# Three transformer blocks on one core: block 1's attention without GpSimd, modulation steps moved, tiles padded to aligned places

## The chip, the cores and the metric

The kernel runs on one core of one Trainium2 chip. The metric is the device time of one execution in microseconds (us). A core has five engines with an instruction queue each, and each works through its queue in order: TensorE (PE, matrix products, with its weight loads shown apart as PEld), VectorE (DVE), ScalarE (ACT), GpSimd (POOL) and SyncE (SP), which here only starts transfers. Transfers run on 16 DMA engines. On-chip memory is SBUF (128 partitions, operands) and PSUM (128 partitions, results of PE).

## The reference

One sequence of 1024 tokens of width 1024 goes through three blocks. The first is the one whose code changes most:

```
h = rmsnorm(x, g_in);  proj = h @ w_in          # q, k, v, u, b, c, q_mem, gate
# sticks-breaking attention, 8 heads of 64:
z = q k^T / 8
A[t,s] = sigmoid(z[t,s]) * prod_{s<j<t} (1 - sigmoid(z[t,j]))     for s < t
y_sb = A v
y_conv = b * causal_conv3(c * u)
y_mem = softmax attention over 256 memory tokens (rmsnorm(mem) @ w_mem_kv)
x = x + (concat(norms of y_sb, y_conv, y_mem) * silu(gate)) @ w_out;  rmsnorm
```

Block 2 modulates its input with six vectors, `ada = silu(c) @ w_ada + b_ada` (a 1024 x 6144 matrix), then mixes with a gated recurrence (HGRN2) and a spatial gating unit, and runs a mixture of 32 experts. Block 3 has 16 more tokens in front, a convolution of width 31 beside a latent attention, and a feed-forward layer of width 2816. All of it is in 32-bit floats.

## The kernel before

Every large product is made of three PE products: each operand is split into a rounded high part (`hi`, cast on ACT, L70) and the rest (`lo`, a subtraction on DVE, L71, on POOL in places), and `mm3` (L76 to L78) adds hi x hi, lo x hi and hi x lo in PSUM. Weights come 128 x 1024 at a time on SP's queue, and are split after landing.

Block 1 runs in stages. The value projection `vproj` comes first, then `heads(0)`, the query and key projections of the first pair of heads. Attention is four passes, j = 0 to 3, of one pair of heads each; a pass has eight query blocks i of 128 rows. For block i, `scores` makes z for both heads in PSUM with n = 128 (i+1) columns; ACT makes 1 - sigmoid (`nb`) and sigmoid (`be`); DVE runs a product scan along the row, backwards (`nb`, L294); POOL multiplies `be` by the shifted scan (L296) after a one-column memset (L293). `attend` then, one block later, transposes the weights on PE (L309), copies them from PSUM to `wt`, on DVE and ACT in turns (L313), and multiplies them with the values (`pv`, L320). After blocks 0, 2, 4 and 6 PE does one half-projection of the next pair of heads (`heads(j + 1)`). At the head of a pass the queries and keys are split (`qs` L85 on DVE, `kk` L93 on POOL). After attention come the convolution (six projections of two halves each, L250 evacuates a half on DVE), the memory attention, the gates, and the output projection.

Modulation of block 2 runs as a background task. One step (`background`) loads a 128 x 512 piece of `w_ada`, 256 KB (L680), and accumulates it on DVE (L711, `acc`); 96 steps make twelve vectors of 512, and after each vector two or eight matmuls close it (L692, L698). `nbg` gives the number of steps before and after each `attend`, 24 for a pass, 96 in all; the loads share SP's queue with the weights, in three buffers, two of them loaded in advance from the head of the program.

The order of each engine's queue is made by the framework's scheduler from the program's order and the buffers, and tiles get their SBUF addresses from pools, one behind the other, so a tile's start address follows from the sizes of the tiles before it.

## Time and profile before

| | us |
|---|---|
| median of three runs (lowest, highest) | 3194.37 (3192.73, 3198.25) |
| the profiled execution, its own time | 3193.8 |
| span in the profile | 3192.1 |
| PE busy, share of the span | 2938.7, 92% |
| DVE busy | 1948.9, 61% |
| ACT busy | 1170.4, 37% |
| POOL busy | 847.8, 27% |

The span reaches from the first to the last recorded instruction; the execution's own time lies 1.7 us above it. Busy times of engines overlap, since the engines run beside each other. In the trace attention lies between about 102 and 391 us, the convolution from 391 to about 460, memory attention and gates up to 619, the output projection to 728, block 2's mixers to about 1245, experts to about 1900, and block 3 to the end, with the feed-forward layer from about 2540.

### The profile page before, as it was taken

What the parts mean: (1) busy time and instruction counts of PE and PEld (TensorE: products, weight loads), DVE (VectorE), ACT (ScalarE), POOL (GpSimd) and SP (SyncE); (2) the same over time, 40 slices, a digit from 0 to 9 for tenths busy, and PEclk for the clock granted to TensorE, in tenths of its full rate; (3) what the DMA queues carried; (4) which work ended last, traced back from release to release, by engine and by line L of the source; (5) the groups of instructions that cost most, each with busy time, mean ns of one, the idle gap of its engine ahead of it and who ended that gap; (6) DMA issues with size and microseconds to landing.
All of it is one profiled execution on the core that took longest, in us unless ns stands there. A gap on an engine that the chain in (4) does not pass through costs nothing. (4 is left out here: it accounts for less than half of the span.)

```text
span 3192.1 us, 47341 instructions
## 1 busy us (share of the span) xinstructions
PE 2938.7 (92%) x18630; PEld 2520.0 (79%) x18630; DVE 1948.9 (61%) x2753; ACT 1170.4 (37%) x2006; POOL 847.8 (27%) x618
## 2 busy tenths in 40 slices
PE   6978799998989886899999599999999999999998
PEld 6755587778777774777777599866699999999997
DVE  5688855662664577564876679786644544444445
ACT  3444426532554212342554443346414222222222
POOL 0333421000544454232433201100103222222221
PEclk9998899999999997899999799999999999999999
DMA  6122221222110244656886511400022111111111
GB/s 221 40 93 92 85 64 62 90 80 70 34 35 21 67 146 165 205 170 196 268 275 225 163 47 49 129 21 21 9 93 68 40 55 50 48 47 40 47 47 60
DMA packets 97038, 298.23 MB, mean 93 GB/s; under 512 B 13556, under 2 KB 17396, under 8 KB 96648
## 3 DMA queue, kind: packets, MB, share of 16 engines
q1 hardware_dynamic: 82200, 246.21, 22.6%
q0 software_dynamic: 8784, 31.99, 4.1%
q10 hardware_dynamic: 5792, 16.54, 1.6%
q8 instruction: 165, 2.70, 0.3%
q14 instruction: 97, 0.79, 0.1%
HBM read 254.61 MB, written 40.08 MB: 92 GB/s over the span
## 5 line engine op out<-in xcount | busy, mean ns | idle before, releaser
L71 DVE TENSOR_TENSOR w_lo<-w_raw,w_hi 128x1024 fp32r<-128x1024 f32 (+3 forms) x134 | 157.6, 1178 | 303.5 <-ACT w_hi L70 303.2
L78 PE MATMUL psu<-f_hi,w_lo 128*128 128x342 f32 x1056 | 337.1, 319 | 0.6 <-DVE w_lo L71 0.6
L70 ACT CAST w_hi<-w_raw 128x1024 fp32r<-128x1024 f32 (+3 forms) x156 | 148.7, 955 | 514.6 <-PE ps L77 179.1
L76 PE MATMUL psu<-f_hi,w_hi 128*128 128x342 f32 x1056 | 337.1, 319 | 0.0
L77 PE MATMUL psu<-f_lo,w_hi 128*128 128x342 f32 x1056 | 337.1, 319 | 0.0
L78 PEld LDWEIGHTS psu<-f_hi,w_lo 128*128 128x128 f32 x1056 | 198.8, 188 | 0.8 <-DVE w_lo L71 0.8
L77 PEld LDWEIGHTS psu<-f_lo,w_hi 128*128 128x128 f32 x1056 | 198.8, 188 | 0.4
L76 PEld LDWEIGHTS psu<-f_hi,w_hi 128*128 128x128 f32 x1056 | 198.6, 188 | 0.4
L1419 DVE TENSOR_TENSOR wlo<-raw,whi 128x1024 fp32r<-128x1024 f32 x120 | 192.8, 1671 | 7.1 <-ACT whi L1365 5.6
L1365 ACT CAST whi<-raw 128x1024 fp32r<-128x1024 f32 x156 | 155.4, 1048 | 49.3 <-DMA raw<-in_w_down 25.1
L1779 DVE SCALAR_TENSOR_TENSOR u<-u,conv_w 128x1040 f32<-128x1040 f32 x120 | 159.9, 1332 | 6.5 <-ACT u L1777 5.1
L77 PE MATMUL ps<-wlo,xhi 128*128 128x512 f32 x400 | 158.0, 395 | 6.2 <-DVE wlo L1419 5.8
L76 PE MATMUL ps<-whi,xhi 128*128 128x512 f32 x400 | 158.0, 395 | 4.6 <-issue 3.1
L78 PE MATMUL ps<-whi,xlo 128*128 128x512 f32 x400 | 157.4, 394 | 0.0
L76 PE MATMUL ps<-hhi,w_hi 128*128 128x512 f32 x384 | 154.3, 402 | 0.0
L77 PE MATMUL ps<-hlo,w_hi 128*128 128x512 f32 x384 | 152.7, 398 | 0.0
L78 PE MATMUL ps<-hhi,w_lo 128*128 128x512 f32 x384 | 152.1, 396 | 0.0
L131 POOL TENSOR_TENSOR w_raw<-w_raw,ffn_norm_g 128x1024 f32<-128x1024 f32 x44 | 87.1, 1982 | 222.8 <-DMA w_raw<-in_w_up 215.8
L2217 DVE TENSOR_TENSOR acc<-acc,psd 128x512 f32<-128x512 f32 x176 | 116.1, 683 | 43.2 <-PE psd L78 41.7
L77 PE MATMUL psd<-w_lo,a_hi 128*128 128x512 f32 x352 | 139.4, 396 | 1.3 <-POOL w_lo L71 1.3
L78 PE MATMUL psd<-w_hi,a_lo 128*128 128x512 f32 x352 | 139.3, 396 | 0.0
L76 PE MATMUL psd<-w_hi,a_hi 128*128 128x512 f32 x352 | 139.1, 396 | 0.0
(614 smaller groups left out, 8071.2 us busy)
## 6 DMA issues: line engine op xcount, KB each, us to landing
raw<-in_w_up SPq DMA_DIRECT2D x104, 512.0 KB, 5.3
w_raw<-in_w_in SPq DMA_DIRECT2D x54, 512.0 KB, 3.7
raw<-in_w_down SPq DMA_DIRECT2D x52, 512.0 KB, 3.9
w<-in_w_ada SPq DMA_DIRECT2D x96, 256.0 KB, 2.8
w_raw<-in_w_up SPq DMA_DIRECT2D x44, 512.0 KB, 3.6
w_raw<-in_w_down SPq DMA_DIRECT2D x22, 512.0 KB, 3.6
w_raw<-in_w_out SPq DMA_DIRECT2D x16, 512.0 KB, 6.5
xk<-in_xT SPq DMA_DIRECT2D x16, 256.0 KB, 6.9
```

Source lines behind the costliest of these rows:

```text
L70: (hi_eng or nc.scalar.copy)(hi, v)
L71: (lo_eng or nc.vector).tensor_sub(lo, v, hi.bitcast(F32))
L76: mm(out, l[0], r[0], start=start, stop=False)
L77: mm(out, l[0], r[1], start=False, stop=False)
L78: mm(out, l[1], r[0], start=False, stop=stop)
L131: nc.gpsimd.tensor_mul(w, w, gain[:, :, None].to_broadcast(sh))
L1365: nc.scalar.copy(self.whi[j], self.raw[j % NR])
L1419: lambda j, *w: (nc.gpsimd if j in (4, 7) else nc.vector).tensor_sub(*w))
L1779: keep(nc.vector.scalar_tensor_tensor(acc, x, w, acc, op0=OP.mult, op1=OP.add))
L2217: nc.vector.tensor_add(acc[t][:, ns], acc[t][:, ns], ps)
```

## The change

Four things change.

- In attention, POOL has no work. DVE multiplies `be` by the scan (L298, one column less, so that no memset is needed) and subtracts for `kk` (L93); ACT makes all copies to `wt` and the zeros of the memory keys.
- `background` is called from other places and takes a number of steps: three for each of the second value projection's row blocks, four after each half-projection of the convolution, two at each half of the gates, the rest at the end. The first loads start after the last value weights instead of at the head; four buffers instead of three.
- The memory tokens are loaded and split (`memory()`) after the first of the convolution's two column groups, not after the convolution.
- Tiles are padded or share a place ("room", "edge", rows of 1152, 1120, 1056 or T + 16 instead of odd lengths). Of the tiles in SBUF 860 of 2404 began at a multiple of 64 bytes before and 2139 of 2400 do now; at a multiple of 512 bytes 287 and now 1461. All 512-column matmuls now read both operands from multiples of 512 bytes; before, only some did: the experts' operands did, `w_hi` of block 1's projections began 384 bytes past one, the down-projection's operands 96 and 128 past, block 2's projections 32 past. The feed-forward chunks become 352, 336 and 338 columns instead of three of 342, in rows of T + 16.

```diff
@@ pair_double
-            self.nc.gpsimd.tensor_sub(lo[h][own], x[own], hi[h][own].bitcast(F32))
+            self.nc.vector.tensor_sub(lo[h][own], x[own], hi[h][own].bitcast(F32))
@@ vproj, and what follows the second half's weights
                     nc.scalar.activation(vt[:, t, g * 256:(g + 1) * 256], ps[:, :256], AF.Copy,
                                          scale=rt[:, t:t + 1])
+                    background(psm, 3 * g)
...
                 wvpart(1, w1, c)
+            background(psm, 0)
@@ proj
-        def proj(m, outs, scale=1.0):
+        def proj(m, outs, scale=1.0, steps=0):
             w = ws.load(a["w_in"][m])
             for hf in range(2):
                 proj_half(w, hf, outs[hf], scale)
+                background(psm, steps)
@@ scores
-                    nb = at.tile([P, T + 1], F32, name="nb", bufs=2)
+                    nb = at.tile([P, T], F32, name="nb", bufs=2)
...
-                    nc.gpsimd.memset(nb[:, n:n + 1], 1.0)
                     nc.vector.tensor_tensor_scan(nb[:, :n][:, ::-1], nb[:, :n][:, ::-1],
                                                  nb[:, :n][:, ::-1], 1.0, op0=OP.mult, op1=OP.bypass)
-                    nc.gpsimd.tensor_mul(be[:, :n], be[:, :n], nb[:, 1:n + 1])
+                    nc.vector.tensor_mul(be[:, :n - 1], be[:, :n - 1], nb[:, 1:n])
@@ attend
-                        eng = nc.scalar.copy if cx.flip % 2 else nc.vector.tensor_copy
-                        cx.flip += 1
-                        eng(wt[:, c * P:(c + nbk) * P], pt[:, :nbk * P])
+                        nc.scalar.copy(wt[:, c * P:(c + nbk) * P], pt[:, :nbk * P])
@@ the passes
                     scores(j, i)
-                    nbg = (0, 0, 1, 2, 2, 2, 2, 3)[i]
-                    for _ in range(nbg):
-                        background(psm)
                     if len(todo) == 1:
                         attend(*todo.pop(0))
                     todo.append((j, i))
-                    for _ in range(nbg):
-                        background(psm)
...
-            background(psm, last=True)
@@ convolution
-                proj(12 + j, halves(u))
-                proj(16 + j, halves(c))
-                proj(14 + j, halves(b))
+                proj(12 + j, halves(u), steps=4)
+                proj(16 + j, halves(c), steps=4)
+                proj(14 + j, halves(b), steps=4)
...
+                if j == 0:
+                    memory()
@@ gates
-                    yield gate(m, hf, gate_of(pl, w, hf))
+                    gt = gate_of(pl, w, hf)
+                    background(psm, 2)
+                    yield gate(m, hf, gt)
...
+            background(psm, 0, last=True)
@@ ada
-                w = pl.tile([P, 512], F32, name="w", bufs=3)
+                w = pl.tile([P, 512], F32, name="w", bufs=4)
...
-        for _ in range(2):
+        for _ in range(3):
             load()
...
-                g = pl.tile([P, 512], F32, name="g", bufs=1)
+                g = pl.tile([P, 512], F32, name="g", tag="w", bufs=4)
@@ placement, a few of many
-    FCH = ((0, 342), (342, 342), (684, 342))
+    FCH = ((0, 352), (352, 336), (688, 338))
...
-        self.fhi = fp.tile([P, 8, T + 2], F32R, name="f_hi")
+        self.fhi = fp.tile([P, 8, T + 16], F32R, name="f_hi")[:, :, :T + 2]
...
+        self.cv.tile([P, 88], F32, name="room")
...
+        edge = es.enter_context(tc.tile_pool(name="edge", bufs=1, side="right")).tile([P, 120], F32, name="edge")
```

What this does to the queues, at three places. First DVE ahead of attention, from the end of the input statistics to the first evacuation of a head's projection. In each row stands the line, the operation, result and operands, the shape, and a count where rows repeat. `wvl` and `w_lo` are weight splits, `kk` zeros. Before:

```order
L711 SCALAR_TENSOR_TENSOR acc<-w,cs,acc 128x512 x4
L71 TENSOR_TENSOR wvl_136<-w_raw,wvh_135 128x1024
L711 SCALAR_TENSOR_TENSOR acc<-w,cs,acc 128x512
L71 TENSOR_TENSOR wvl_136<-w_raw,wvh_135 128x1024
L711 SCALAR_TENSOR_TENSOR acc<-w,cs,acc 128x512 x3
L71 TENSOR_TENSOR w_lo<-w_raw,w_hi 128x1024
L711 SCALAR_TENSOR_TENSOR acc<-w,cs,acc 128x512
L71 TENSOR_TENSOR w_lo<-w_raw,w_hi 128x1024
L711 SCALAR_TENSOR_TENSOR acc<-w,cs,acc 128x512 x7
L273 TENSOR_SCALAR kk<-ones 64x1024 x2
L250 SCALAR_TENSOR_TENSOR x<-ps,rb 128x512
```

The same stretch of DVE's queue after the change (the steps are now L718, evacuations L252):

```order
L718 SCALAR_TENSOR_TENSOR acc<-w,cs,acc 128x512 x3
L71 TENSOR_TENSOR wvl_131<-w_raw,wvh_130 128x1024 x2
L718 SCALAR_TENSOR_TENSOR acc<-w,cs,acc 128x512 x4
L71 TENSOR_TENSOR w_lo<-w_raw,w_hi 128x1024
L718 SCALAR_TENSOR_TENSOR acc<-w,cs,acc 128x512
L71 TENSOR_TENSOR w_lo<-w_raw,w_hi 128x1024
L718 SCALAR_TENSOR_TENSOR acc<-w,cs,acc 128x512 x16
L276 TENSOR_SCALAR kk<-ones 64x1024 x2
L718 SCALAR_TENSOR_TENSOR acc<-w,cs,acc 128x512 x7
L252 SCALAR_TENSOR_TENSOR x<-ps,rb 128x512
L718 SCALAR_TENSOR_TENSOR acc<-w,cs,acc 128x512
```

There were 16 steps ahead of the first evacuation; now there are 31, and one behind it.

Second, DVE in attention, in query blocks 5 to 7 of a pass (the scan is printed as SCALAR_TENSOR_TENSOR on `nb`). Before:

```order
L294 SCALAR_TENSOR_TENSOR nb<-nb 128x768
L313 COPY wt<-ps 128x512
L294 SCALAR_TENSOR_TENSOR nb<-nb 128x768
L313 COPY wt<-ps 128x512
L294 SCALAR_TENSOR_TENSOR nb<-nb 128x896
L313 COPY wt<-ps 128x512
L294 SCALAR_TENSOR_TENSOR nb<-nb 128x896
L313 COPY wt<-ps 128x512
L711 SCALAR_TENSOR_TENSOR acc<-w,cs,acc 128x512 x6
L250 SCALAR_TENSOR_TENSOR x<-ps,rb 128x512
L711 SCALAR_TENSOR_TENSOR acc<-w,cs,acc 128x512
```

The same blocks after:

```order
L296 SCALAR_TENSOR_TENSOR nb<-nb 128x768
L298 TENSOR_TENSOR be<-be,nb 128x767
L296 SCALAR_TENSOR_TENSOR nb<-nb 128x768
L298 TENSOR_TENSOR be<-be,nb 128x767
L296 SCALAR_TENSOR_TENSOR nb<-nb 128x896
L298 TENSOR_TENSOR be<-be,nb 128x895
L296 SCALAR_TENSOR_TENSOR nb<-nb 128x896
L298 TENSOR_TENSOR be<-be,nb 128x895
```

Each scan is now followed by its multiplication, and copies and steps are gone from DVE's queue.

Third, DVE in the convolution, second column group, after the change (`L403`, `L406` are the taps, `ms` the split of the memory tokens):

```order
L71 TENSOR_TENSOR w_lo<-w_raw,w_hi 128x1024
L718 SCALAR_TENSOR_TENSOR acc<-w,cs,acc 128x512 x4
L252 SCALAR_TENSOR_TENSOR c<-ps,rb 128x512
L718 SCALAR_TENSOR_TENSOR acc<-w,cs,acc 128x512 x4
L252 SCALAR_TENSOR_TENSOR c<-ps,rb 128x512
L71 TENSOR_TENSOR w_lo<-w_raw,w_hi 128x1024
L403 TENSOR_SCALAR acc<-cu,conv_w,conv_b 128x1024
L406 SCALAR_TENSOR_TENSOR acc<-cu,conv_w,acc 128x1024 x2
L718 SCALAR_TENSOR_TENSOR acc<-w,cs,acc 128x512
L252 SCALAR_TENSOR_TENSOR b<-ps,rb 128x512
L718 SCALAR_TENSOR_TENSOR acc<-w,cs,acc 128x512
L388 SCALAR_TENSOR_TENSOR ms<-mt,g_mem,ms 128x256
```

Before, this stretch held the weight splits, evacuations and taps alone; now about four steps stand ahead of each evacuation. Over the whole program 32 steps stand ahead of attention, none in it, and of the other 64 some 47 in the convolution and the projection after it and 17 at the gates.

## Rows read from the trace of the kernel before

**Rows 1.** The page of the whole run: the span, the busy time of each engine with its share of the span and its instructions, and PE's busy share in 40 equal slices in tenths.

```profile
span 3192.1 us, 47341 instructions
...
PE 2938.7 (92%) x18630; PEld 2520.0 (79%) x18630; DVE 1948.9 (61%) x2753; ACT 1170.4 (37%) x2006; POOL 847.8 (27%) x618
...
PE   6978799998989886899999599999999999999998
```

**Rows 2.** Busy time by stretch of time. Columns: stretch in us, its length, then for PE, PE's weight loads, DVE, ACT and POOL the busy time with the number of instructions, the mean granted clock of PE, the busy share of the DMA engines, GB/s.

```profile
14.00:46.00 32.00, 23.65 (x156) 23.07 (x157) 21.45 (x32) 11.51 (x19) 1.07 (x2) 0.89 0.77 260
46.00:79.00 33.00, 30.93 (x241) 30.25 (x241) 17.16 (x24) 9.39 (x17) 1.02 (x1) 0.95 0.57 193
14.00:79.00 65.00, 54.58 (x395) 53.31 (x396) 38.60 (x55) 20.91 (x36) 2.09 (x3) 0.92 0.67 226
79.00:102.00 23.00, 23.00 (x105) 18.78 (x104) 7.25 (x10) 6.95 (x12) 2.68 (x3) 1.00 0.07 24
102.00:391.00 289.00, 231.97 (x1458) 170.88 (x1456) 243.59 (x224) 130.73 (x242) 122.50 (x152) 0.92 0.26 84
391.00:460.00 69.00, 69.00 (x298) 55.83 (x297) 27.12 (x24) 7.80 (x10) 9.63 (x6) 1.00 0.15 46
460.00:500.00 40.00, 36.48 (x215) 31.78 (x214) 28.57 (x42) 24.35 (x43) 17.06 (x15) 1.00 0.38 120
2540.00:3192.00 652.00, 642.04 (x3598) 595.46 (x3597) 306.27 (x347) 144.66 (x214) 156.54 (x77) 1.00 0.15 48
```

**Rows 3.** Groups of instructions by line, DVE, 102 to 391 us. Columns: line, engine, operation, result and operands with shapes, count, busy us and mean ns of one, idle time before them and what ended it.

```profile
L294 DVE TENSOR_TENSOR_SCAN nb<-nb 128x128 f32<-128x128 f32 (+7 forms) x64 | 112.1, 1763 | 5.9 <-ACT nb L291 5.7
...
L711 DVE SCALAR_TENSOR_TENSOR acc<-w,cs,acc 128x512 f32<-128x512 f32 x80 | 81.4, 1022 | 12.4 <-DMA w<-in_w_ada 11.4
...
L313 DVE COPY wt<-ps 128x512 f32<-128x512 f32 (+3 forms) x48 | 28.7, 601 | 0.9 <-PE pv L320 0.6 <-PE ps L309 0.3
...
L85 DVE TENSOR_TENSOR qs<-x,qs 64x512 fp32r<-64x512 f32 x12 | 13.7, 1143 | 0.4
```

**Rows 4.** The same for POOL and ACT, 102 to 391 us.

```profile
L296 POOL TENSOR_TENSOR be<-be,nb 128x128 f32<-128x128 f32 (+7 forms) x64 | 90.3, 1415 | 132.0 <-DVE nb L294 72.7 <-ACT qs L84 18.0 <-ACT be L292 17.5
...
L313 ACT COPY wt<-ps 128x128 f32<-128x128 f32 (+3 forms) x48 | 20.6, 435 | 30.3 <-issue 13.2 <-PE ps L309 7.7 <-PE pv L320 5.0
```

**Rows 5.** Waits, 102 to 391 us. Columns: who waited, and for whose instruction; total us, times, longest.

```profile
POOL be L296 <- DVE nb L294: 72.7, 33, 8.6
...
PE ps L309 <- DVE wt L313: 22.8, 10, 3.6
...
PE pv L320 <- DVE wt L313: 20.4, 20, 2.3
...
PE ps L309 <- POOL be L296: 6.1, 6, 1.5
```

**Rows 6.** Instructions in order of time on DVE, and one of POOL, in the last pass of attention. Columns: start and length in us, engine, line, operation.

```profile
356.35 1.74 DVE L294 TENSOR_TENSOR_SCAN nb<-nb 128x768 f32<-128x768 f32 x1
...
358.26 1.88 POOL L296 TENSOR_TENSOR be<-be,nb 128x768 f32<-128x768 f32 x1 [2.23 <-DVE nb L294]
...
358.66 3.09 DVE L294 TENSOR_TENSOR_SCAN nb<-nb 128x768 f32<-128x768 f32 x1
...
363.94 2.01 DVE L294 TENSOR_TENSOR_SCAN nb<-nb 128x896 f32<-128x896 f32 x1
```

**Rows 7.** All scans of the stage: shortest, median and longest in ns, first and last start in us.

```profile
L294 DVE TENSOR_TENSOR_SCAN nb<-nb x64: 397/1617/3786, 104.2 to 377.0; 128x128 f32<-128x128 f32 x8, 128x256 f32<-128x256 f32 x8, 128x384 f32<-128x384 f32 x8, 128x512 f32<-128x512 f32 x8
```

**Rows 8.** Groups of instructions by line and shape, DVE, 14 to 102 us.

```profile
L711 DVE SCALAR_TENSOR_TENSOR acc<-w,cs,acc 128x512 f32<-128x512 f32 x16 | 12.0, 751 | 7.7 <-DMA w<-in_w_ada 7.3 <-DMA acc<-in_b_ada 0.2
...
L71 DVE TENSOR_TENSOR wvl<-w_raw,wvh 128x1024 fp32r<-128x1024 f32 x4 | 4.9, 1223 | 4.9 <-ACT wvh L70 4.9
...
L85 DVE TENSOR_TENSOR qs<-x,qs 64x512 fp32r<-64x512 f32 x4 | 2.7, 686 | 0.8 <-ACT qs L84 0.7
```

**Rows 9.** Groups by line, PE, 102 to 391 us: the matmuls that close a modulation vector.

```profile
L692 PE MATMUL ps<-acc,ones 128*128 128x512 f32 x16 | 10.9, 771 | 2.6 <-ACT wt L313 2.6
L698 PE MATMUL ps<-ones,acc 128*128 128x128 f32 x32 | 4.3, 276 | 0.0
```

**Rows 10.** Groups by line, DVE, 391 to 460 us (convolution).

```profile
L385 DVE SCALAR_TENSOR_TENSOR acc<-cu,conv_w,acc 128x1024 f32<-128x1024 f32 x4 | 5.1, 1284 | 0.1
...
L250 DVE SCALAR_TENSOR_TENSOR c<-ps,rb 128x512 f32<-128x512 f32 x4 | 2.8, 692 | 16.8 <-PE ps L78 16.8
```

**Rows 11.** Matmuls on one tile in a short stretch in which PE never pauses, one row for each of the three products that follow each other in turn (of some groups one row is shown). Columns: line, operands, count, shortest/median/longest ns, start of the first and of the last in us.

```profile
L78 PE MATMUL psy<-whi,alo x12: 389/389/389, 1494.7 to 1502.2; 128*128 128x512 f32 x12
...
L76 PE MATMUL psd<-w_hi,a_hi x15: 393/395/398, 2933.9 to 2943.7; 128*128 128x512 f32 x15
...
L78 PE MATMUL ps<-hhi,w_lo x15: 390/392/404, 391.6 to 401.4; 128*128 128x512 f32 x15
...
L78 PE MATMUL ps<-h2hi,w_lo x11: 395/395/396, 782.8 to 789.8; 128*128 128x512 f32 x11
...
L77 PE MATMUL o<-wo,yhi x15: 387/395/397, 654.8 to 664.6; 128*128 128x512 f32 x15
...
L76 PE MATMUL psu<-f_hi,w_hi x56: 314/319/327, 2903.8 to 2929.7; 128*128 128x342 f32 x56
```

**Rows 12.** DMA issues on the page: what is loaded, by which queue, count, KB of each, median us from issue to landing.

```profile
w<-in_w_ada SPq DMA_DIRECT2D x96, 256.0 KB, 2.8
```

More of the change, by code (lines that the diff above doesn't have):

```diff
@@ L2375, in body, with background @@
                     ada = b2.ada(ea, gates)
-                    next(ada)
-                    def background(psm, last=False):
-                        try:
-                            ada.send(psm)
-                            while last:
+                    begun = []
+                    def background(psm, n, last=False):
+                        if not begun:
+                            begun.append(next(ada))
+                        try:
+                            while n or last:
                                 ada.send(psm)
+                                n -= 1
                         except StopIteration:
```

106 lines of the change are left out of this document (55 added, 51 removed).

## The prediction, made before the changed kernel was run

> **What bounds it now.** The page of the whole run first [rows 1]: TensorE (PE) is busy 92% of the span and VectorE 61%, and the slices of PE fall well under nine tenths in a few places only; one is slices 1 to 5 (6, 9, 7, 8, 7), block 1. Then the table by stage [rows 2]. Convolution and feed-forward hold PE at 69.00 of 69.00 us and 642 of 652: only shorter PE work can shorten them. Attention is different: in 289 us PE is busy 232 (57 idle), VectorE (DVE) 243.6, ScalarE (ACT) 130.7, GpSimd (POOL) 122.5. DVE there holds the 64 scans (112.1 us), 80 modulation steps (81.4) and 48 of the 96 copies of transposed weights (28.7) [rows 3]; POOL holds the 64 multiplications (90.3) and ACT the other copies [rows 4]. The waits say how this costs PE: 22.8 + 20.4 us behind copies on DVE and 6.1 behind POOL's products, and POOL itself waits 72.7 for scans [rows 5]. The copies are short; they are late because DVE's queue puts scans and steps ahead of them. The rows in order of time show more [rows 6]: a 128x768 scan alone takes 1.74 us, the next, beside POOL's multiplication, 3.09. So the scans' 112.1 us hold time lost to POOL.
>
> **The change, part by part.**
>
> *Attention.* DVE's new load in the stage starts from 243.6. Out go the steps (81.4) and the copies (28.7). For scans beside no POOL work, I take a straight line through the shortest of all scans, 0.40 us at 128 columns, and the undisturbed 1.74 at 768 [rows 6, 7]: 2.09 ns a column, 0.13 us fixed, so 0.40 to 2.27 for 128 to 1024 columns, 10.7 per head and 85.5 for 64: 27 less. The 12 qs splits measured 1143 ns each here and 686 in the quieter opening (1143: 13.7 us over 12) [rows 3, 8]: 5 less. In come 64 multiplications with two inputs. Their nearest row is the weight split of the same kind, 128x1024 in 1.22 us, and the 64x512 split in 0.686 [rows 8]: 1.05 ns a column and 0.15 fixed, 0.29 to 1.22, 6.0 per head, 48 in all. Also 14 kk splits from POOL at 0.69: 10. DVE: 243.6 - 81.4 - 28.7 - 27 - 5 + 48 + 10 = 159.5. ACT: 130.7 + 36 copies of 0.59 + some 4.6 for the 12 smaller ones, less 5 of modulation outputs, 152. PE: 232 less the matmuls that close a modulation vector, 10.9 + 4.3 [rows 9], 217. DVE is no longer the fullest engine; PE is.
>
> How long then? The 217 were measured at a mean granted clock of 0.92 [rows 2], with tails of matmuls that stood alone; if half of the missing 8% comes back, 208. Of the 57 us idle, 43 were behind DVE's copies and 6 behind POOL; what is left are the other 8 and new waits for scan, multiplication and copy in a row, for which I take 9: 17 together. Stage: 225, gain 64. Bounds: all the clock back, 200, and 5 idle, 205 (gain 84); the clock unchanged and 33 idle, 250 (gain 39).
>
> *Modulation steps.* 96 steps of 0.75 us and 256 KB. In the order of after, 32 stand ahead of attention (16 before), none in it, 48 in the convolution and 16 at the gates. Their cover: each convolution half-projection is 24 matmuls, 5.6 us of PE at 69.00 us for 298 [rows 2]; DVE has four steps (3.0), one evacuation (0.69), half a split (0.6) and a share of the convolution's taps (5.1 over 12 halves, 0.4) [rows 10], under 5 us: it fits, narrowly. The transfers are 4x256 + 256 KB for 5.6 us, 235 GB/s, where the opening moved 260 GB/s with its DMA engines busy 0.77 [rows 2]. So DVE and DMA both come near PE there; what is queued behind a late step is the evacuation of a projection, whose PSUM buffer PE wants two halves later, and the weight split that PE wants next. In the opening, 24 steps in the second value projection (192 matmuls, 25 us of PE at the 30.93 us for 241 of its stretch [rows 2]) need 6.3 MB plus weights. I take 5 us for all such stalls; below: 0, all hidden; above 25, where transfers run only at the 226 GB/s of the opening's mean: convolution with its 1.25 MB a half and 2 MB of memory tokens would take 12 x 1.31 + 2.1 = 17.8 MB / 226 = 79 us, 10 over, and as much again ahead of attention plus 5 at the gates. The closing matmuls (15 us of PE at most) move from a stage where PE idles to stages where it is full: +9, between 5 and 15 (steps that close beside the attention's ends or in PE's opening gaps cost nothing).
>
> *Start and memory tokens.* Two step loads leave the head of SP's queue, 0.5 MB where 260 GB/s flow and PE idles 10.4 of 65 us [rows 2]: -2. Splitting the memory tokens during the convolution takes away the 3.5 us of PE idle in 460 to 500: -3, and puts some 5 us on DVE in the convolution, part of the stalls above.
>
> *Placement.* The page's durations hide it, so I went to start times of matmuls that follow each other without a gap, 512 columns wide [rows 11]. Experts (psy; both operands at multiples of 512 bytes): 7.5 us from first to last of 12 rows, 33 matmuls on, 0.227 each. Feed-forward down (psd; its operands at 96 and 128 past such a multiple): 9.8 over 42, 0.233. Block 1 (hhi, weights at 384): 9.8 over 42, 0.233, and 69.00 / 298 = 0.2315 in its longest stretch. Block 2 (h2hi): 7.0 over 30, 0.233; output projection: 0.233. What differs between the two groups is the start address, and after the change all of them have the experts' placement. By the program's counts, 864 matmuls of block 1's projections stand outside attention: 864 x 5 ns = 4.5. h2hi 768 x 6 = 4.6, half of it in a stage that PE bounds: 2.3. Output projection: 3. psd 1056 x 6.2 = 6.5. Feed-forward up has 25.9 us over 165 matmuls of 342 columns, 0.157; its new chunks, 352, 336 and 338, hold the same columns, and rows that now start at multiples of 64 bytes rather than anywhere may shift each by -1.6 to +1.3 ns: 3168 matmuls, -5 to +4, taken as 0. Sum -16; bounds 0, if something else sets the two spacings, and -25.
> The Trainium skill speaks against this part: TensorE: Matmul & The Clock Gate, section Back-to-back issue gap, gives a spacing that depends on the number of columns alone, N/2.4 + 2.5 ns, 216 for 512. By it the placement would be worth nothing, and the sum 16 us less. The trace does not agree with one figure for one width: 227 and 233 stand beside each other.
>
> **Sum.** -64 + 5 + 9 - 5 - 16 = -71. The profiled execution took 3193.8 (span 3192.1 and 1.7 around it): 3122.8. It lies 0.6 below the median of the runs, 3194.4, so about 3123.
>
> **Rivals.**
> *Attention stays a chain.* Scan and multiplication now run on one engine, one behind the other (2.27 + 1.22 for each head at full length, 7 us for two), and PE may wait as large a share as now: 217 / (232/289) = 270, gain 19 instead of 64: 3168. For it: every head's weights pass from ACT to DVE to PE to ACT before PE can use them. Against: one query block took 7.6 us (356.35 to 363.94) with POOL, steps and copies between its scans [rows 6], and DVE has 21 us less per pass, (243.6 - 159.5) / 4.
> *Placement is worth nothing:* 3139. For it: between the experts and the others not only the addresses differ, the loops around the matmuls do too. Against: psd, hhi and h2hi stand in loops as different from each other and all show 0.233. The section of the Trainium skill's TensorE: Matmul & The Clock Gate named above says as much as this rival.
> *Steps bind the transfers* in the convolution and the opening: +20 on top, 3143.
> *The other side: a step queue that starves PE.* Each step waits for its own load, four slots deep. If the loads did not overlap, a step would cost its landing time and itself, 2.8 + 0.75 = 3.55 us [rows 8, 12]; 80 steps ahead of evacuations would be 284 us against 25 + 23 + 69 of PE cover (second value projection, first heads, convolution), 167 over: 3290, slower. It decides where 80 steps cost 117 + 71 = 188, 2.35 us each. Against it: the 16 steps of the opening waited 7.7 us in all, 0.5 each, with three slots [rows 8].
> That no steps are left in attention is certain from the order, so that the change does nothing is no case.
>
> **Chances.** The forecast 0.70; attention a chain 0.10; placement nothing 0.09; transfers bind 0.07; starved 0.04. The low end is the forecast with attention at 84 and placement at 25 without any stall, 3123 - 20 - 9 - 5 = 3089, rounded down: 3085; the high end reaches the rival of the chain, 3168. The likeliest case's own range is 3095 to 3150. A difference under 0.2%, 6 us, can't be told from none: faster 0.94, same 0.02, slower 0.04, since every case but the last stays over 20 us ahead.
>
> **What would show it.** Right: attention (first z matmul to last pv) near 225 us, PE its fullest engine, scans of 1024 columns all near 2.27 us, no wait of PE on wt by DVE; convolution still PE-full at 69 to 75 us with its steps; psd, hhi and h2hi spaced 0.227. Wrong: an attention over 250 us with PE waiting for be or wt; PE idle in the convolution with DVE waiting for the steps' transfers; spacings still 0.233.

## The result, and the profile after

The changed kernel takes 3117.19 us (median of four runs, 3116.41 to 3122.47) where the kernel before took 3193.76 beside it: a ratio of 0.9759, 95% interval 0.9745 to 0.9773. The forecast was 3123 in a range of 3085 to 3168. The profiled execution was the longest of the four, 3122.47 us, with a span of 3120.8.

The page of the changed kernel, the same lines as in [rows 1], and the granted clock by slice:

```profile
span 3120.8 us, 47239 instructions
...
PE   7999999989898895999997899999999999999998
...
PEclk9999999999999997999998899999999999999999
```

Its busy time by stretch (columns as in [rows 2]); the stretches are the heads' projections, attention, the convolution, the memory keys and values, gates, and feed-forward:

```profile
76.00:99.00 23.00, 23.00 (x109) 19.23 (x108) 16.70 (x23) 7.19 (x12) 0.00 (x0) 1.00 0.54 175
99.00:311.00 212.00, 201.23 (x1410) 152.56 (x1409) 165.12 (x174) 144.47 (x279) 0.13 (x2) 1.00 0.06 19
311.00:393.00 82.00, 79.99 (x347) 64.78 (x348) 63.21 (x76) 16.65 (x30) 16.41 (x14) 0.98 0.55 176
393.00:430.00 37.00, 32.00 (x185) 28.85 (x183) 26.27 (x36) 19.82 (x32) 10.58 (x8) 0.91 0.38 118
430.00:552.00 122.00, 121.02 (x668) 95.72 (x669) 84.05 (x167) 78.86 (x135) 10.04 (x10) 1.00 0.30 94
2465.00:3120.00 655.00, 645.55 (x3641) 603.65 (x3639) 311.77 (x357) 145.62 (x214) 160.87 (x79) 1.00 0.16 49
```

Attention went from 288.3 us (first z matmul to last pv matmul) to 212.0; PE is busy 201.2 of 212, at a granted clock of 1.00 where it had been 0.92, and DVE's load fell to 165.1 although it took on 64 products. DVE's groups in that stretch, and ACT's copies (columns as in [rows 3]):

```profile
L296 DVE TENSOR_TENSOR_SCAN nb<-nb 128x128 f32<-128x128 f32 (+7 forms) x64 | 86.2, 1352 | 7.1 <-ACT nb L294 6.8
L298 DVE TENSOR_TENSOR be<-be,nb 128x127 f32<-128x127 f32 (+7 forms) x64 | 48.1, 757 | 7.5 <-ACT ym L324 0.5
...
L85 DVE TENSOR_TENSOR qs<-x,qs 64x512 fp32r<-64x512 f32 x12 | 8.2, 686 | 0.4
...
L313 ACT COPY wt<-ps 128x512 f32<-128x512 f32 (+3 forms) x96 | 40.9, 506 | 13.5 <-PE ps L311 12.7 <-PE pv L320 0.6
```

The 64 scans take 86.2 us instead of 112.1, and the longest of all 2.29 instead of 3.79 us:

```profile
L296 DVE TENSOR_TENSOR_SCAN nb<-nb x64: 400/1352/2285, 102.6 to 303.8; 128x128 f32<-128x128 f32 x8, 128x256 f32<-128x256 f32 x8, 128x384 f32<-128x384 f32 x8, 128x512 f32<-128x512 f32 x8
```

Copies keep PE waiting once, for 1.8 us; what is left of [rows 5] is small (who waited, for whom; us in all, times, longest):

```profile
PE z L97 <- ACT be L295: 2.9, 8, 0.6
...
PE ps L311 <- DVE be L298: 2.3, 6, 0.7
PE ps L311 <- ACT wt L313: 1.8, 1, 1.8
```

From the traces of both kernels the length of each stage on PE, in us, worked out from the first and last matmuls of each ("after, again" is a second profile of the changed kernel):

| stage | before | after | after, again |
|---|---|---|---|
| up to the first z matmul | 101.9 | 98.9 | 100.2 |
| attention | 288.3 | 212.0 | 212.1 |
| to the first memory-key matmul | 90.5 | 96.8 | 97.2 |
| to the output projection | 138.5 | 144.8 | 144.7 |
| to block 2 | 109.0 | 106.8 | 106.7 |
| block 2 up to the end of the experts | 1057.7 | 1053.6 | 1052.9 |
| block 3, up to its attention | 265.3 | 264.7 | 266.6 |
| block 3's attention | 260.0 | 267.0 | 262.2 |
| to the first up-projection | 125.4 | 126.7 | 126.3 |
| first up- to first down-projection | 91.4 | 91.9 | 91.4 |
| down- and other up-projections | 654.7 | 648.2 | 648.2 |

So attention gives 76, the convolution and the gates give 12.6 back, the output projection gains 2 and the feed-forward layer 6.5. The rest moves by a few us either way from execution to execution; block 3's attention, 7 longer in the first profile, is looked at below.

### The profile page after: what moved, and what is told of

Its sections match the earlier page's. It is cut to its first block, busy times and chain, and to the rows that moved or that the text cites. A ratio compares the mean times of both kernels' runs of the same rounds, so it can differ in the third digit from the quotient of the medians.

```text
span 3120.8 us, 47239 instructions
## 1 busy us (share of the span) xinstructions
PE 2917.5 (93%) x18630; PEld 2522.0 (81%) x18630; DVE 1927.6 (62%) x2785; ACT 1194.9 (38%) x2061; POOL 728.4 (23%) x471
## 5 line engine op out<-in xcount | busy, mean ns | idle before, releaser
L71 DVE TENSOR_TENSOR w_lo<-w_raw,w_hi 128x1024 fp32r<-128x1024 f32 (+2 forms) x134 | 155.5, 1162 | 299.4 <-ACT w_hi L70 299.0
L78 PE MATMUL psu<-f_hi,w_lo 128*128 128x338 f32 (+2 forms) x1056 | 337.8, 320 | 0.0
L77 PE MATMUL psu<-f_lo,w_hi 128*128 128x338 f32 (+2 forms) x1056 | 337.8, 320 | 0.0
L76 PE MATMUL psu<-f_hi,w_hi 128*128 128x338 f32 (+2 forms) x1056 | 337.3, 319 | 0.0
```

The costliest lines, as they stand in the source:

```text
L71: (lo_eng or nc.vector).tensor_sub(lo, v, hi.bitcast(F32))
L76: mm(out, l[0], r[0], start=start, stop=False)
L77: mm(out, l[0], r[1], start=False, stop=False)
L78: mm(out, l[1], r[0], start=False, stop=stop)
```

## The experiments

**Which part of attention's change does it?** First the engine changes alone, on the kernel before.

```diff
+ nc.vector.tensor_mul(be[:, :n - 1], be[:, :n - 1], nb[:, 1:n])   # was on gpsimd, n columns
+ nc.scalar.copy(wt[...], pt[...])                                 # was vector and scalar in turns
+ self.nc.vector.tensor_sub(lo[h][own], ...)                       # was on gpsimd
```

> The kernel before with only the engine changes of attention: products and kk on VectorE, copies on ScalarE. Steps, memory tokens and placement as before. Theory: VectorE now has 244 - 29 - 27 - 5 + 48 + 10 = 241 us in the stage, as much as it had, but copies no longer stand behind scans and steps; the stage takes 255 to 275 us against 289, the whole 3160 to 3180. Rival (GpSimd and the copies were all of it): 212 to 225 and 3117 to 3130 less the 16 of placement, 3133 to 3146.

Measured: 3158.72 us, ratio 0.9895 (0.9877 to 0.9913); attention 249.5 us. Busy time of this run's attention, columns as in [rows 2], and below it its groups on DVE:

```profile
99.00:348.00 249.00, 220.78 (x1448) 163.22 (x1448) 215.12 (x253) 150.07 (x289) 5.38 (x12) 0.96 0.30 97
```

```profile
L293 DVE TENSOR_TENSOR_SCAN nb<-nb 128x128 f32<-128x128 f32 (+7 forms) x64 | 85.5, 1348 | 1.6 <-ACT nb L291 1.3
L708 DVE SCALAR_TENSOR_TENSOR acc<-w,cs,acc 128x512 f32<-128x512 f32 x79 | 58.4, 741 | 11.8 <-DMA w<-in_w_ada 11.0
L295 DVE TENSOR_TENSOR be<-be,nb 128x127 f32<-128x127 f32 (+7 forms) x64 | 47.4, 750 | 2.8
```

The time lies just under what was expected and attention 5 us under it. What that expectation had wrong is DVE's load, 215 instead of 241: not the scans alone but the modulation steps, too, had been slowed by GpSimd's work, from 741 ns to 1022 [rows 3], 58.4 us for 79 of them instead of 81.4 for 80. The trace of before says the same within one stage: counted from the starts, 39 of its 80 steps ran beside no GpSimd instruction and took 750 ns in the mean, and the other 41 took 1281.

Then the reverse, the changed kernel with the old engines.

```diff
+ nc.gpsimd.memset(nb[:, n:n + 1], 1.0)
+ nc.gpsimd.tensor_mul(be[:, :n], be[:, :n], nb[:, 1:n + 1])
+ eng = nc.scalar.copy if cx.flip % 2 else nc.vector.tensor_copy
+ self.nc.gpsimd.tensor_sub(lo[h][own], ...)
```

> The changed kernel with its engines in block 1 put back: GpSimd multiplies be by the scan, clears the extra column and subtracts for kk; copies to wt go to VectorE and ScalarE in turns. The modulation steps stay out of attention. Theory (steps, copies, and the scans' slowing by GpSimd all cost): VectorE in attention carries 244 - 81 = 163 us, scans 112 again; PE waits behind copies on VectorE and for GpSimd's products; the stage takes 240 to 260 us where the changed kernel takes 212, the whole 3145 to 3165. Rival (the steps alone were the cause): 212 to 220 us and 3117 to 3125.

Measured: 3160.22, ratio 0.989 (0.9873 to 0.9906); attention 257.2 us, inside the expectation. This run's scans in attention, and below them PE's waits there:

```profile
L297 DVE TENSOR_TENSOR_SCAN nb<-nb 128x128 f32<-128x128 f32 (+7 forms) x64 | 119.8, 1883 | 14.0 <-ACT nb L294 13.6
```

```profile
PE pv L323 <- DVE wt L316: 18.5, 12, 1.9
PE ps L312 <- POOL be L299: 12.0, 11, 1.9
```

So of the 76.3 us the engines alone give 38.8 and moving the steps (with the padding) 31.1; together 6 more than their sum. Neither is "the" cause, and both rivals fall: the one by which the steps were all of it, and the one by which GpSimd and the copies were. Two runs take the engine changes apart. Only the products back on GpSimd:

> The changed kernel with one thing put back: GpSimd multiplies be by the scan (and clears the extra column). Copies to wt stay on ScalarE, kk on VectorE, steps out of attention. Theory (GpSimd slows the scans beside it, and its products come late): scans near 112 us in all instead of 86, VectorE 165 - 48 + 26 = 143 us in the stage, so it is less full than now and still PE waits more: the scan, then a product of up to 2 us on GpSimd, follow each other across two engines; attention 222 to 240 us instead of 212, the whole 3128 to 3146. Rival (VectorE's load alone counts): attention 205 to 212, the whole 3111 to 3118.

Measured: 3139.08, ratio 0.9826 (0.9808 to 0.9843); attention 230.9 us, as expected. Its groups of scans, kk splits and products there, and below them PE's wait:

```profile
L297 DVE TENSOR_TENSOR_SCAN nb<-nb 128x128 f32<-128x128 f32 (+7 forms) x64 | 93.5, 1495 | 40.5 <-ACT nb L294 40.3
L93 DVE TENSOR_TENSOR kk<-x,kk 64x512 fp32r<-64x512 f32 x14 | 19.7, 1406 | 0.4
...
L299 POOL TENSOR_TENSOR be<-be,nb 128x128 f32<-128x128 f32 (+7 forms) x64 | 101.5, 1586 | 138.0 <-DVE nb L297 76.3 <-ACT be L295 19.5 <-PE z L288 18.9
```

```profile
PE ps L312 <- POOL be L299: 13.2, 15, 2.8
```

The wait is the expected one, PE for GpSimd's products, 13.2 us. The scans were slowed less than thought, to 93.5 and not 112, while the 14 kk splits took 19.7 us where the changed kernel has 9.6. Why the scans were slowed less is not shown: counted from the traces, 47 of the 64 ran beside GpSimd's work here, hardly fewer than the 54 of the run with all engines back, where they took 119.8. DVE, emptier, sat 40.3 us waiting for the next sigmoid. Only the copies back, on both engines in turns:

> The changed kernel with another thing put back: copies to wt go to VectorE and ScalarE in turns, products stay on VectorE. Theory (a copy on VectorE waits in its queue behind two scans and two products, up to 7 us, and PE waits for it): VectorE 165 + 29 = 194 us in the stage; attention 222 to 242 us, PE waiting some 20 us for wt by VectorE; the whole 3128 to 3148. Together with putting back the products this should not exceed the 45 us that all engines put back cost, unless both together cost more than their sum. Rival (copies are short, 29 us in all, and cost nothing): 212 to 216.

Measured: 3149.78, ratio 0.9861 (0.9843 to 0.9879), a little above the expected band; attention 245.0. Its busy time there, and below it PE's waits for copies:

```profile
100.00:342.00 242.00, 210.32 (x1376) 158.37 (x1376) 184.44 (x221) 123.49 (x228) 0.13 (x2) 0.94 0.06 17
```

```profile
PE pv L322 <- DVE wt L315: 8.5, 15, 1.0
...
PE ps L311 <- DVE wt L315: 6.3, 11, 0.7
```

The waits for copies on DVE are there, 14.8 us, less than the 20 that were expected; the rest of the 33 us has other parts: the granted clock is 0.94 in this stretch and not 1.00, with PE's busy time at 210 and not 201. Why the clock fell to 0.94 here and only to 0.98 with the products was not settled. Putting back products (19) and copies (33) costs more singly than both with kk together (45). That each alone already makes PE wait for a part of what the other would is a reading of these sums, and no run shows it.

**What is placement worth, and by which rule?** All padding taken out of the changed kernel (the "room", "edge" and longer rows; chunks of 342).

> The changed kernel with all padding taken out (the modulation, memory and attention changes stay, the feed-forward chunks are 342 again). The tiles' start addresses change: the experts' two operands both begin 480 bytes past a multiple of 512, block 1's projections read their moving operand at 480 and their weights at 352 or 448, block 2's likewise, the down-projection 96 and 128. Theory (a matmul of 512 columns takes 233 ns whenever an operand's start is off a multiple of 512): all of these show 0.233, the experts too, and the kernel is slower than the changed one by 1152 x 5 + 768 x 6 + 768 x 5 + 1056 x 6 + 1800 x 6 ns, 31 us, of which the stages that PE bounds show 20 to 28: 3137 to 3145. Rival 1 (only the two operands' places relative to each other count): the experts stay at 0.227, slower by 12 to 17: 3129 to 3134. Rival 2 (placement is worth nothing): 3117, spacings unchanged.

Measured: 3125.41, ratio 0.9787 (0.9771 to 0.9803), 7.4 us over the changed kernel's 3118.01 in the same comparison. The experts' second product (psy), block 1's projections (hhi) and the down-projection (psd), in stretches without a pause (columns as in [rows 11]):

```profile
L76 PE MATMUL psy<-whi,ahi x12: 389/389/487, 1472.1 to 1479.7; 128*128 128x512 f32 x12
...
L78 PE MATMUL ps<-hhi,w_lo x15: 390/393/404, 350.0 to 359.8; 128*128 128x512 f32 x15
...
L76 PE MATMUL psd<-w_hi,a_hi x32: 393/396/397, 2861.6 to 2883.3; 128*128 128x512 f32 x32
```

The experts, with both operands 480 bytes past a multiple of 512, keep 389 ns a matmul and 7.6 us over 33 matmuls, 0.230, with one pause in it; the median from start to start is 0.227, as in the changed kernel. hhi, whose moving operand begins at 480 and whose weights at 352, 128 bytes apart, shows 9.8 over 42, 0.233, and psd, 32 bytes apart, 21.7 over 93, 0.233. The rule that the prediction rested on, starts at multiples of 512, falls; rival 1, the two places relative to each other, stands. Its price does not: 7.4 and not 12 to 17. The 7.4 are rough, too, since the executions of the two kernels nearly meet (3121.5 to 3129.2 and 3114.4 to 3121.0); the stages say more. The feed-forward stage lengthened by the expected 6.5 us (648.2 to 654.7) and the stretches from attention's end to the output projection by 2.0 (97.5 + 146.4 against 97.2 + 144.7), while block 2 up to the end of the experts became shorter, 1048.4 where the changed kernel has 1053.6 and 1052.9, for a reason that was not found.

The output projection is not in this price. Without padding its two operands both begin at 480 bytes, and its matmuls keep the changed kernel's spacing, 7.5 us over 33, 0.227, in a stretch of the run without padding:

```profile
L78 PE MATMUL o<-wo,ylo x12: 389/389/393, 639.8 to 647.3; 128*128 128x512 f32 x12
```

So the 2 us that this stage gained over the kernel before come on top.

How the spacing goes with width and place was then mapped: the up-projections took their weights at eight places in turns, and cut their columns in five ways.

```diff
+ w = ws.load(a["w_up_3"][m], gain=fg, off=16 * (self.ups % 8))
+ for c0, n in MAPS[self.ups // 8 % 5]:      # 352+336+338, 3x342, 384+384+258, 512+256+258, 320+320+386
```

> One look at what the start addresses do to the spacing of matmuls: the changed kernel, whose feed-forward up-projections take their weights at 0, 64, 128, ... 448 bytes past a multiple of 512 in turns, and cut their 1026 columns in five ways in turns (352+336+338, 3 x 342, 384+384+258, 512+256+258, 320+320+386); rows of the moving operand are 4352 bytes apart, so their places relative to the weights go in steps of 256. The run without padding showed that at 512 columns only the two operands' places relative to each other count: equal 227, 32 apart 233 or 234, 384 apart 232. Theory: for each width some relative places give less than the mean of 14.5 ns over columns / 2.4 GHz, and equal places are best only at 512; the spread over places is 5 to 12 ns, and the same for all matmuls with the same width and places. Rival: equal places are best at every width; then the widths 256 and 384 are at their lowest there. No time is expected of this kernel: 3105 to 3130.

Two stretches of 512 columns and two of 256 (the shortest, median and longest of the duration say it too), at equal places and 64 bytes apart:

```profile
L76 PE MATMUL psu<-f_hi,w_hi x8: 389/389/389, 2751.7 to 2756.5; 128*128 128x512 f32 x8
...
L76 PE MATMUL psu<-f_hi,w_hi x9: 277/394/395, 2762.6 to 2767.8; 128*128 128x512 f32 x8, 128*128 128x258 f32 x1
...
L78 PE MATMUL psu<-f_hi,w_lo x8: 283/283/389, 2756.9 to 2759.5; 128*128 128x256 f32 x7, 128*128 128x512 f32 x1
...
L78 PE MATMUL psu<-f_hi,w_lo x8: 276/276/394, 2768.3 to 2770.8; 128*128 128x256 f32 x7, 128*128 128x512 f32 x1
```

A matmul of 512 columns lasts 389 ns at equal places and 394 at 64 bytes; one of 256 columns 283 and 276, the other way round. Worked out from the starts of all up-projection matmuls in this trace, the mean spacing in ns beyond columns / 2.4, a line to measure from, by the distance of the two operands' starts:

| columns | 0 or 256 bytes | 64 or 320 | 128 or 384 | 192 or 448 |
|---|---|---|---|---|
| 256 | 13.0 | 7.1 | 12.2 | 6.6 |
| 258 | 13.2 | 13.2 | 14.3 | 11.2 |
| 320 | 13.3 | 13.3 | 13.3 | 13.3 |
| 342 (first chunk) | 15.3 | 11.0 | 17.0 | 14.8 |
| 384 | 13.9 | 14.9 | 15.5 | 13.3 |
| 512 | 13.4 | 20.0 | 19.0 | 16.1 |

Distances 256 bytes apart agree to 0.3 ns. Equal places are the best at 512 columns and the worst at 256, so the theory stands in its main point and its rival falls; the spread of 5 to 12 ns that it named is there at 256, 342 and 512 columns, and not at 258, 320 and 384. The whole took 3119.92 in its single run.

A version was made from that table: quarters.

```diff
- FCH = ((0, 352), (352, 336), (688, 338))
+ FCH = ((0, 256), (256, 256), (512, 256), (768, 258))
+ w = ws.load(a["w_up_3"][m], gain=fg, off=16)        # 64 bytes; moving rows 4224 bytes apart
```

> A version made from the map of spacings: the changed kernel with the feed-forward up-projection cut into 256 + 256 + 256 + 258 columns instead of 352 + 336 + 338, its weights 64 bytes past a multiple of 512 and its moving rows 4224 bytes apart, so that the two operands always stand 64 or 192 bytes apart in a period of 256. The map showed 256 columns at 113 or 114 ns there (120 at equal places) and 258 at 119.7; four chunks then cost 3 x 113.5 + 119.7 = 460 ns where the three of the changed kernel cost 162 + 154 + 155 = 471. Theory: 11 x 1056 = 11.9 us less in a stage that PE fills: 3105 to 3108 against 3117 or 3118, from the first to the last of the down-projections 648.2 less some 10.4, 638. Rival 1 (four evacuations instead of three, and one more change of PSUM buffer, give it back): 3115 to 3120. Rival 2 (weight loads bind when short matmuls follow each other): spacing 117 or more, 3118 to 3140.

Measured: 3126.33, ratio 0.978 (0.9764 to 0.9796): no gain, and if anything some 8 us slower than the changed kernel. One stretch of its up-projections, columns as in [rows 11]:

```profile
L77 PE MATMUL psu<-f_lo,w_hi x9: 279/280/280, 2899.7 to 2902.5; 128*128 128x256 f32 x9
```

Nine rows, 24 matmuls: 2.8 us, 0.117 each, and not the map's 0.1135. What differs is that here the distance changes from 64 to 192 bytes and back with every contraction step, as rows are 4224 bytes apart, while in the map it stayed the same from matmul to matmul. That a distance must hold over a stream to give its spacing was not tried here (rows of 4352 bytes would have cost one of the six buffers of output weights, as in the map), and another run speaks against it as the whole cause: the one with the shifted value-projection weight below. Four chunks at 0.117 cost what three cost before, and up to the first down-projection 7 us more were lost.

**Where do 12.6 us go after attention?** Without the steps' loads and accumulations:

```diff
- load()
- nc.vector.scalar_tensor_tensor(acc, ws.pop(0), cs[:, k:k + 1], acc, op0=OP.mult, op1=OP.add)
```

> The changed kernel without the 96 loads and accumulations of the modulation (left out: the product silu(c) @ w_ada; the vectors hold the bias alone). The twelve closing groups of matmuls stay where they are. The stretch from the end of attention to the memory keys grew by 6.3 us with the change and that from there to the output projection by 6.3. Theory (about 7 of these 12.6 are closing matmuls that PE now runs where it is full, the rest waits for steps and for weights whose loads stand behind steps' loads): 5 to 7 us less after attention, and 1 to 4 less ahead of it: 3108 to 3112. Rival 1 (closing matmuls are all): 3115 to 3118. Rival 2 (the loads cost more than seen, by slowing others): below 3106.

Measured: 3127.25, but that total tells nothing of the steps: without the modulation other experts are chosen, and their stage took 517.2 us instead of 494.6. The two stretches can be read, since they lie before it: 94.3 and 137.5 us, where the changed kernel has 97.2 and 144.7. The busy time of this run there:

```profile
310.00:404.00 94.00, 92.98 (x412) 75.71 (x412) 42.88 (x47) 25.14 (x43) 22.39 (x19) 1.00 0.20 61
404.00:541.00 137.00, 135.51 (x788) 109.94 (x787) 84.41 (x165) 90.31 (x154) 11.87 (x11) 1.00 0.21 64
```

PE is busy 135.5 of 137 here; in the changed kernel it idled 2 us in the convolution, for an evacuation on DVE, and 5 of 37 us at 393 to 430, at a granted clock of 0.91, first of all for a weight of the memory keys, in PE's waits in the two stretches:

```profile
PE ps L76 <- DVE b L252: 2.0, 1, 2.0
...
PE ps L76 <- ACT w_hi L70: 3.5, 1, 3.5
```

What held that weight up stands in the changed kernel's second profile, where the wait is 3.2 us, in the order of time on DVE and ACT (columns as in [rows 6]):

```profile
410.41 2.33 DVE L718 SCALAR_TENSOR_TENSOR acc<-w,cs,acc 128x512 f32<-128x512 f32 x3
412.66 0.68 DVE L252 SCALAR_TENSOR_TENSOR x<-ps,rb 128x512 f32<-128x512 f32 x1
...
413.37 1.26 ACT L84 CAST qm<-x 64x512 fp32r<-64x512 f32 x2 [4.26 <-DVE x L252]
414.65 1.04 ACT L70 CAST w_hi<-w_raw 128x1024 fp32r<-128x1024 f32 x1
```

The transfer of the weight had been issued by 394.95. Its cast stood on ACT behind the cast of the memory queries, which waited 4.26 us for an evacuation on DVE, and ahead of that evacuation stood three steps.

So 10 of the 12.6 us hang on loads and accumulations. The closing matmuls, which this run keeps, take 7.5 us of PE in the two stretches, worked out from their starts; that this run is only 2.8 us above the kernel before there (231.8 against 229.0) is because the shorter spacing and the memory keys' old idle time work the other way. Ahead of attention it was shorter by 2 to 4 us (96.4 against 98.9 and 100.2), but that stretch moves by as much from execution to execution.

The steps that the convolution could not absorb were thus still in DVE's queue when evacuations and weights behind it were due. That suggests fewer of them there. One run had it beside the quarters and a shifted value-projection weight:

> The same, and two small things: the value projection's weights, its moving operand, stand 64 bytes past a multiple of 512, so that its 384 matmuls of 256 columns come every 113 or 114 ns instead of 120; and the convolution takes three modulation steps behind each half instead of four, the gates three instead of two. Theory: 384 x 6.3 = 2.4 us less, of which the opening, which also waits for transfers, shows about 1; the stretch from the end of attention to the memory keys 97 falls to 94 to 96, that to the output projection stays at 144 to 147: 3101 to 3107. Rival (more steps at the gates hold up the weights there as they did in the convolution): 3106 to 3112.

Measured: 3117.08, ratio 0.9751 (0.9735 to 0.9766): above the expectation, for the quarters still cost; but the two stretches fell to 91.2 and 141.3. The shifted weight brought nothing that shows: the first z matmul came at 101.5 us. Its matmuls of 256 columns stand a steady 64 bytes apart and yet came every 117 to 119 ns, where the changed kernel has 120 and the map 113 or 114. They last 279 ns, near the 280 of the quarters and above the 276 of the map:

```profile
L78 PE MATMUL ps<-wvh,hlo x39: 279/279/280, 59.8 to 75.0; 128*128 128x256 f32 x39
```

So at 256 columns something besides the distance and its steadiness sets the spacing, and the runs do not say what. Then the steps alone:

```diff
- proj(12 + j, halves(u), steps=4)      # and the other two projections
+ proj(12 + j, halves(u), steps=3)
- background(psm, 2)                    # at the gates
+ background(psm, 3)
```

> The changed kernel with one change of numbers: three modulation steps behind each half of the convolution instead of four (36 instead of 48) and three at each half of the gates instead of two (36 instead of 24). In the run that had this beside other changes the stretch from the end of attention to the memory keys fell from 97 to 91 us with PE never idle, and that to the output projection from 145 to 141. Theory (steps that outrun their cover late in the convolution hold up evacuations and weights, and PE then also shows a lower granted clock): the same here, 9 to 10 us less, everything else as in the changed kernel: 3106 to 3110. Rival (the shorter stretch came from the other edits there): 3115 to 3119.

Measured: 3106.53, ratio 0.9722 (0.9709 to 0.9735), below the changed kernel's interval of 0.9745 to 0.9773: the fastest of all, and faster than both kernels. It came out 10.7 below the changed kernel, of which the two stretches show 8.8 (91.2 and 141.6 where there were 96.8 and 144.8). Its convolution, and the rest up to the output projection:

```profile
311.00:406.00 95.00, 94.99 (x442) 78.52 (x438) 65.58 (x80) 25.03 (x43) 24.45 (x17) 1.00 0.42 135
406.00:550.00 144.00, 141.12 (x795) 113.05 (x796) 109.53 (x209) 96.39 (x166) 14.43 (x14) 1.00 0.41 129
```

PE is busy 94.99 of 95 us, at a full clock. One step further:

> The same further: two steps behind each half of the convolution (24) and four at each half of the gates (48). Theory: the convolution has no more to give, PE is full there with three, so it shows only two closing groups of matmuls less, about 2 us, and the gates take them and have VectorE at 118 of 141 us instead of 106: 3106 to 3112 in all. Rival 1 (fewer steps still help): 3100 to 3105. Rival 2 (the gates' steps now hold up their evacuations): 3113 to 3125.

Measured: 3113.28, ratio 0.9749 (0.9735 to 0.9764), just above the theory's range and inside the second rival's; its executions, 3109.2 to 3118.1, do not tell the two apart. The convolution's stretch is 90.3, little less, and the gates' 143.7, two more than with three: the two stretches together are 1.2 us longer than with three. In the profiled executions both kernels end within 4 us of each other, and the lowest and highest times, 3101.3 to 3116.6 and 3109.2 to 3118.1, overlap: that three is better than two is likely and not certain.

**Does block 3 pay?** The changed kernel again:

> The changed kernel once more. In its first profile block 3's attention (from the first of its score matmuls to the last of its value matmuls) took 267 us against 260 of the kernel before, though nothing of its code changed, and that execution was some 5 us above the other three. Theory: chance of that one execution; then the stage takes 259 to 261 here, and the whole 3116 to 3118. Rival: the new placement costs those 6 us there; then 266 to 268 again, and the whole 3117 as well, with the placement's gain smaller than worked out.

Measured: 3118.01, ratio 0.9758 (0.9741 to 0.9774), block 3's attention 262.2: neither the theory nor its rival as put. The stage took 260.0 and 259.8 us in the two kernels that keep the steps in attention, and 261.9 to 267.3 in all others, the one without padding (264.5) among them, so placement is not what lengthens it. What goes with it is the granted clock, in the busy time of that stretch: first the kernel before, then the changed kernel in its first profile, then the run without padding (columns as in [rows 2]):

```profile
2051.00:2311.00 260.00, 244.44 (x1803) 170.34 (x1804) 179.38 (x485) 134.81 (x341) 17.61 (x28) 0.97 0.10 25
```

```profile
1977.00:2244.00 267.00, 251.09 (x1807) 174.88 (x1807) 179.47 (x485) 135.04 (x342) 17.57 (x28) 0.94 0.10 24
```

```profile
1976.00:2240.00 264.00, 248.68 (x1800) 172.59 (x1802) 179.51 (x485) 134.31 (x341) 17.57 (x28) 0.95 0.10 25
```

Its work is the same in all of them; why the clock is 0.97 in two kernels and 0.94 to 0.96 in the rest stays open.

## Why the prediction was right, step by step

*Attention, right in its mechanism and 13 us too small.* The terms of DVE's new load came out nearly one by one: scans 86.2 (85.5 foretold), products 48.1 (48), qs splits 0.686, kk splits 9.6 (10), in all 165 (159.5); ACT 144.5 (152). PE is the fullest engine, as foretold. The term that was mis-sized is the time that the stage takes beside PE's work: I gave half of the missing clock back and 17 us of idle; the trace shows the full clock, 1.00, PE busy 201 and 11 idle. The stage is 212 and not 225, inside the bounds of 205 and 250.

*What the trace of before could have told and I did not read:* 80 steps at a mean of 1022 ns [rows 3] beside 751 in the opening [rows 8]. GpSimd slowed the steps as it slowed scans and splits; I used that comparison for the qs splits alone. The sum would have stayed as it is, since the steps left the stage at their measured 81.4; it is the expectation of the engines alone that went wrong by it. The Trainium skill has it as a rule (SBUF — State Buffer, section Who interferes with whom): a DVE instruction with two SBUF inputs contends with a GpSimd instruction that reads SBUF. The traces agree: 741 ns without GpSimd's products, 1022 with them; the scans 1.35 and 1.76 us in the mean.

*Steps and closing matmuls, right in their mechanism, the stalls half the size.* 5 + 9 - 3 = 11 were foretold and 12.6 measured, but the 12.6 already hold the shorter spacing in the same stretches, some 2 us. The closing matmuls take 7.5 us of PE where I had 9. What was mis-sized are the stalls, 10 us on loads and accumulations where I had 5. And I had taken the memory stage's 3.5 us of idle as saved: another wait of 3.5 us stands in its place. The sentence that put DVE near PE in the convolution and named the evacuation behind a late step was the right one: one evacuation, behind three steps and the split of the memory tokens, held PE up by 2 us within the convolution (1 us in the run without steps), and another, behind three steps, held up the cast of a memory keys' weight.

*Placement, half the size and by another rule.* The sum had 16; the run without padding gives 7.4, and the output projection, which that run leaves as it is, 2 more. The feed-forward layer has 6.5 of it, just as worked out. That spacing falls to 0.227 came true for psd, hhi, h2hi and the output projection, by the median of each (of the 512-column matmuls only 8 closing ones and 24 of block 3's scores still read an operand off a multiple of 512 bytes); the down-projection of the changed kernel, columns as in [rows 11]:

```profile
L76 PE MATMUL psd<-w_hi,a_hi x29: 389/389/400, 2865.4 to 2884.4; 128*128 128x512 f32 x29
```

19.0 us over 84 matmuls, 0.226. The term that was mis-sized is the price of the shorter spacing outside the feed-forward layer: in block 1 and block 2 it brought 2 us and nothing measurable where I had 4.5 and 2.3, and in the output projection 2 where I had 3. And the reason, multiples of 512, was wrong: the distance counts. The Trainium skill's TensorE: Matmul & The Clock Gate, section Back-to-back issue gap, has N/2.4 + 2.5 ns for a matmul by itself, the figure that the prediction quoted, and for streams of weight load and matmul some 131 ns at 512 columns; neither depends on places. The traces agree with neither: their streams lie 6.6 (256 columns) to 20 ns above N/2.4, by width and distance, and at 512 columns never under 13 in the mean.

*The feed-forward chunks* were taken as 0, and up to the first down-projection the stage shows 91.4, 91.9 and again 91.4.

So a gain of 71 in the profiled execution, and of 77 in the medians, came out where 71 was foretold. The mechanism of the largest term was right; that the total was met to the microsecond in the profiled execution is luck: attention was 12 better, placement some 6 worse, and that execution lost 7 us in block 3's attention, for which no term stood. No rival came true. The one on the other side, steps that starve PE, exists on the scale of 10 us; ahead of attention the 32 steps waited 7.0 us for their loads, 0.2 each, which with their own 0.75 makes under 1 us a step, far from the 2.35 from which it would have decided (the changed kernel's steps up to its attention, columns as in [rows 3]):

```profile
L718 DVE SCALAR_TENSOR_TENSOR acc<-w,cs,acc 128x512 f32<-128x512 f32 x32 | 24.0, 751 | 12.3 <-DMA w<-in_w_ada 7.0 <-DMA acc<-in_b_ada 4.6
```

## What to carry to other kernels

Where two engines both look busy, price each instruction at its undisturbed duration from a quieter stretch of the same trace; the difference shows what a second engine working beside it costs, and what leaves with that engine. Background work should be spread by what each stretch's engines have left after their own work, with a look at what is due right behind it: one step less per half of the convolution, done at the gates instead, was worth some 10 us here. The padding paid its worked-out price here only where the matmul stream was the bound, in the feed-forward layer.

## What the runs showed of the hardware

- The spacing of back-to-back matmuls goes with the distance between the starts of the moving operand and of the weights; in the map it repeats every 256 bytes. At 512 columns it is 0.2267 us at equal places and up to 0.2333; at 256 columns 0.1197 at equal places and 0.1133 to 0.1138 at 64 or 192 bytes; at 320 columns there is no difference. In two other streams of 256 columns, 64 or 192 bytes apart, it was 0.117 to 0.118, so the distance is not all that counts.
- DVE instructions with two inputs in SBUF ran 1.4 to 1.8 times as long beside GpSimd's products: a 128x768 scan 1.74 and 3.09 us [rows 6], a step 0.741 us without them and 1.022 in the mean of a stage with them.
- The granted clock of a stretch moved with how PE was fed, though not strictly: in attention 0.92 with PE busy 232 of 289 us, 0.94 at 210 of 242, 0.95 at 217 of 257 (all engines back), 0.96 at 221 of 249, 0.98 at 205 of 230 (products back), 1.00 at 201 of 212; at 393 to 430 us 0.91 with 32 of 37, and 1.00 at 94.99 of 95 in the convolution with three steps. But block 3's attention, with the same work throughout, had 0.94 to 0.97, for a reason that was not found.
